# High and low parts of one layer's weights: from engine copies to casting and adding transfers

## The chip, the core and the metric

The kernel runs on one core of a Trainium2 chip. Five engines work beside each other, each through its own list of instructions in order: TensorE (PE in the profile, PEld for its weight loads), VectorE (DVE), ScalarE (ACT), GpSimd (POOL) and SyncE (SP), which here only starts DMA transfers. Semaphores hold an instruction back until what it needs is done. The metric is the device time of one execution in microseconds.

## The reference

A trunk of two layers on x of 512 tokens by 1024 channels, float32. Each layer adds a mixer's output to x and then a squared-ReLU MLP's.

```python
def reference(x, ...):
    for layer in range(2):
        h = rmsnorm(x, norm_mix_g[layer])
        if layer % 2 == 0:
            mix = even_mixer(h, ...)   # S5 state space + dilated window attention
        else:
            mix = mlstm_mixer(h, ...)
        x = x + mix
        h = rmsnorm(x, norm_mlp_g[layer])
        x = x + jnp.square(jax.nn.relu(h @ mlp_w1[layer])) @ mlp_w2[layer]
    return x

def even_mixer(h, w_in, ..., w_glu, q_g, k_g, w_out):
    proj = h @ w_in                       # 1024 x 2048: u, q, k, v of 512 each
    y_a = s5_mixer(u, ..., w_glu)         # ends in y * sigmoid(y @ w_glu), 512 x 512
    y_b = dilated_attention(rotary(rmsnorm(q)), rotary(rmsnorm(k)), v)
    return concatenate([y_a, y_b]) @ w_out   # 1024 x 1024
```

## The kernel before

Products with weights are taken in the type float32r, whose mantissa is shorter than that of float32. To keep the accuracy, both factors are split: a high part, which is the number cast to float32r, and a low part, the rest, also cast. Each product is then three matmuls, high by high, high by low and low by high (`mm3`, line 172). Activations are split by `prep` and the like, weights by the functions below.

All weights come as units of 128 x 1024 numbers (512 KB), in the order of use (`unit_list`, line 1271). Units 0 to 25 belong to the even layer: 0 to 15 are the input projection (four each of u, v and the two kinds of q and k steps), 16 and 17 the S5 gate, 18 to 25 the output projection (`out_proj`, line 424). From unit 26 on come the first MLP, the odd layer and the second MLP; some of these units are sums that `t_sums` makes on the way. A unit feeds 24 matmuls with 512 columns.

`w_next` hands out unit `wi` and calls `w_pump` before and after. `w_pump` starts the raw load of up to three units ahead by SP (`w_dma`, tile `wr`, three buffers) and splits up to two ahead: ACT copies raw to high (`wh`, line 160), DVE subtracts high from raw to give low (`wl`, line 161). There are two pairs of high and low buffers. When the even layer's pools are closed, a further pool `wp2` opens (line 1262), with a third pair, and both distances grow by one.

The even layer follows a list of steps written out by hand (`EVEN_SEQ`, line 30): u, v, a, b are projections, n and r norm and rotary of q and k, C, K, E, T, B, O, G parts of the S5 layer for one of four groups, h attention steps, X and Y the end of S5 and the gate. `s5_params` (line 488) first makes tables on DVE, with 26 and more small products by Pool (line 543, tiles `rA`, `s_pr`, `s_la` ...). Pool also takes a power for each q or k norm (line 800) and starts eight transfers a group that spread S5 matrices into the tile `DT` (line 678). A list scheduler then reorders the whole within what the data and the buffers allow, so the order on an engine differs from that of the code.

The lines that hold a unit's way before the change are these; the functions stand in full below.

```python
self.copy_act(h, r)                  # ACT: high part, cast by the output's type
self.sub(l, r, h.bitcast(F32))       # DVE: low part
```

Of the kernel before, what the change touches and what calls it, by code (L numbers as in the profile page):

```python
# [9 lines left out]
F32 = mybir.dt.float32  # L10
F32R = mybir.dt.float32r
I32 = mybir.dt.int32
AF = mybir.ActivationFunctionType
ALU = mybir.AluOpType
AX = mybir.AxisListType

P = 128
# [44 lines left out]
class Trunk:  # L62
# [67 lines left out]
            self.nc.sync.dma_start(out=self.dbg[name], in_=ap)  # L130


    AHEAD_DMA = 3
    AHEAD_SPLIT = 2
    RAW_BUFS = 3
    MORE_DMA = 1

    def w_init(self, units):
        self.wp2 = None
        self.units, self.wi, self.wd, self.wsx = units, 0, 0, 0  # L140
        self.raw, self.split = {}, {}

    def w_dma(self, n):
        while self.wd < n:
            r = self.t(self.wp, (P, 1024), "wr", F32, self.RAW_BUFS)
            u = self.units[self.wd]
            self.dma(r, u() if callable(u) else u)
            self.raw[self.wd] = r
            self.wd += 1

    def w_pump(self):
        n = 0 if self.wp2 is None else 1
        self.w_dma(min(self.wi + self.AHEAD_DMA + n * self.MORE_DMA, len(self.units)))
        while self.wsx < min(self.wi + self.AHEAD_SPLIT + n, len(self.units)):
            r = self.raw.pop(self.wsx)
            third = self.wp2 is not None and self.wsx % 3 == 2
            pool, bufs = (self.wp2, 1) if third else (self.wp, 2)
            h = self.t(pool, (P, 1024), "wh", F32R, bufs)
            l = self.t(pool, (P, 1024), "wl", F32R, bufs)
            self.copy_act(h, r)  # L160
            self.sub(l, r, h.bitcast(F32))
            self.split[self.wsx] = (h, l)
            self.wsx += 1

# [1060 lines left out]
    def run(self):  # L1225
        nc = self.nc
        a = self.a
        self.x = [None] * KT
        self.prm = self.c((P, 3, 32), "prm")
        self.dma(self.prm, a["s5_par"])  # L1230
        self.x_load([0])
        self.gain = self.c((P, 4, KT), "gain")
        self.w_init(self.unit_list())
        self.w_dma(1)
        self.dma(self.gain, a["gain"])
        self.x_load(range(1, 5))
        cst = self.c((P, P + 24), "cst")
        self.dma(cst, a["cst"])
        self.x_load(range(5, 8))
        self.ident, self.onec, self.bones, self.sgn = cst[:, 0:P], cst[:, P:P + 1], cst[:, P + 1:P + 5], cst[:, P + 5:P + 6]  # L1240
        self.hm, self.eye = cst[:, P + 6:P + 8], cst[:, P + 8:P + 24]
        self.w_dma(2)
        self.s5d = self.c((P, 4, 2), "s5d")
        self.dma(self.s5d, a["s5d"])
        qkg = self.c((P, 4), "qkg")
        self.dma(qkg, a["qkg"])
        rot = self.c((P, 2, T), "rot")
        self.dma(rot, a["rot"])
        self.cos, self.sin = rot[:, 0], rot[:, 1]
        self.ts(qkg[:, 0:2], qkg[:, 0:2], 0.125, ALU.mult)  # L1250
        self.qkg = qkg
        self.pwh = self.c((P, 4, 4), "pwh")
        nc.gpsimd.memset(self.pwh, -0.5)
        self.dp = self.ctx.enter_context(self.tc.tile_pool(name="dp", bufs=1, space=bass.MemoryType.DRAM))
        self.hp = self.ctx.enter_context(self.tc.tile_pool(name="hp", bufs=1))
        self.hg = [None] * KT
        self.tq = {}

        self.even()
        if self.stop == "l0mix":  # L1260
            return self.finish()
        self.wp2 = self.ctx.enter_context(self.tc.tile_pool(name="wp2", bufs=1))
        self.mlp(0)
        if self.stop == "l0":
            return self.finish()
        self.odd()
        if self.stop == "l1mix":
            return self.finish()
        self.mlp(1)
# [129 lines left out]
```

## Time and profile before

| | |
|---|---|
| median of 3 runs | 1186.29 us (1185.99 to 1187.22) |
| profiled execution | 1185.93 us, span 1184.1 us |
| PE busy | 1161.5 us, 98% |
| DVE, ACT, POOL busy | 813.4, 643.1, 64.1 us |
| granted TensorE clock | 0.995 of 2.4 GHz in the mean |
| DMA | 216.56 MB, mean 183 GB/s |

The span runs from the first instruction to the last; the profiled execution's own time is 1.83 us longer. A busy PE may hold pipelined matmuls: one of 512 columns shows about 0.39 us, while the next starts 0.23 us after it. What counts is the stretches in which PE waits, and what ended them.

### The profile page before, as it was taken

What the parts mean: (1) busy time and instruction counts of PE and PEld (TensorE: products, weight loads), DVE (VectorE), ACT (ScalarE), POOL (GpSimd) and SP (SyncE); (2) the same over time, 40 slices, a digit from 0 to 9 for tenths busy, and PEclk for the clock granted to TensorE, in tenths of its full rate; (3) what the DMA queues carried; (4) which work ended last, traced back from release to release, by engine and by line L of the source; (5) the groups of instructions that cost most, each with busy time, mean ns of one, the idle gap of its engine ahead of it and who ended that gap; (6) DMA issues with size and microseconds to landing.
All of it is one profiled execution on the core that took longest, in us unless ns stands there. A gap on an engine that the chain in (4) does not pass through costs nothing.

```text
span 1184.1 us, 15701 instructions
## 1 busy us (share of the span) xinstructions
PE 1161.5 (98%) x5540; PEld 956.2 (81%) x5540; DVE 813.4 (69%) x1466; ACT 643.1 (54%) x1162; POOL 64.1 (5%) x121
## 2 busy tenths in 40 slices
PE   6989999999999999999999999999999999999998
PEld 5868776788888888888888888887888888888887
DVE  8799864666457447779858975865664574477796
ACT  5467777444434446666656645544444444456664
POOL 0522220000000000000100000000000000000000
PEclk9989999999999999999999999999999999999999
DMA  6434531359999335565624333222599994346654
GB/s 236 125 95 122 143 79 58 121 202 370 351 345 357 122 120 160 194 195 172 188 90 153 107 108 107 81 89 72 182 353 367 345 350 144 111 157 195 208 185 158
DMA packets 73869, 216.56 MB, mean 183 GB/s; under 512 B 16888, under 2 KB 17992, under 8 KB 73792
## 3 DMA queue, kind: packets, MB, share of 16 engines
q1 hardware_dynamic: 72576, 214.27, 53.7%
q0 software_dynamic: 1216, 1.31, 0.5%
q8 instruction: 43, 0.70, 0.2%
q14 instruction: 34, 0.28, 0.1%
HBM read 175.14 MB, written 38.31 MB: 180 GB/s over the span
## 4 chain that ended last, share of the span: by engine, by line
PE 92%; DVE 3%; ACT 1%; POOL 1%; issue 1%; DMA 1%; SPq 0%; DVEq 0%; ACTq 0%
PE acc L123 79%; PE psa L123 8%; PE psb L123 3%; DVE wl L96 1%; PE psb L898 1%; POOL rA L543 1%; PE psb L281 1%; ACT wh L120 0%; ACT hg L117 0%; DVE hg L108 0%; DMA hg<-in_amask 0%; DMA wr<-in_w_l 0%; DVE x L108 0%; PE psb L1207 0%; DVE x L96 0%
## 5 line engine op out<-in xcount | busy, mean ns | idle before, releaser
L123 PE MATMUL acc<-hg,wh 128*128 128x512 f32 x1600 | 500.7, 393 | 8.8 <-ACT hg L117 7.2
L120 ACT ACTIVATE wh<-wr 128x1024 fp32r<-128x1024 f32 x243 | 257.2, 1060 | 398.1 <-PE acc L123 321.3
L96 DVE TENSOR_TENSOR wl<-wr,wh 128x1024 fp32r<-128x1024 f32 x243 | 297.3, 1224 | 221.5 <-ACT wh L120 211.4
L123 PEld LDWEIGHTS acc<-hg,wh 128*128 128x128 f32 x1600 | 298.7, 188 | 70.1 <-ACT hg L117 7.2
L123 PE MATMUL acc<-hg,wl 128*128 128x512 f32 x800 | 313.6, 392 | 0.6 <-DVE wl L96 0.6
L123 PE MATMUL acc<-wh,sp 128*128 128x512 f32 x768 | 223.0, 389 | 0.0
L123 PEld LDWEIGHTS acc<-hg,wl 128*128 128x128 f32 x800 | 150.7, 188 | 31.9 <-DVE wl L96 1.1
L123 PEld LDWEIGHTS acc<-wh,sp 128*128 128x128 f32 x768 | 144.2, 188 | 30.0
L123 PE MATMUL acc<-wl,sp 128*128 128x512 f32 x384 | 135.9, 390 | 0.8 <-DVE wl L96 0.8
L120 ACT ACTIVATE sp<-s 128x256 fp32r<-128x256 f32 x224 | 89.8, 409 | 6.8 <-PE acc L123 5.7
L96 DVE TENSOR_TENSOR tq<-tq,tq 128x1024 f32<-128x1024 f32 x64 | 78.2, 1222 | 21.0 <-DMA tq<-in_w2s 20.0
L96 DVE TENSOR_TENSOR sp<-s,sp 128x256 fp32r<-128x256 f32 x224 | 86.8, 417 | 1.4 <-ACT sp L120 1.4
L123 PEld LDWEIGHTS acc<-wl,sp 128*128 128x128 f32 x384 | 71.9, 188 | 16.6 <-DVE wl L96 1.6
L123 PE MATMUL acc<-wh,hg 128*128 128x512 f32 x192 | 63.0, 402 | 5.4 <-ACT wh L120 5.4
L123 PEld LDWEIGHTS acc<-wh,hg 128*128 128x128 f32 x192 | 36.6, 193 | 13.2 <-ACT wh L120 5.8
L123 PE MATMUL psa<-wh,sp 128*128 128x512 f32 x128 | 42.0, 389 | 0.0
L117 ACT ACTIVATE rr<-acc 128x512 f32<-128x512 f32 x72 | 41.6, 578 | 0.0
L117 ACT ACTIVATE s<-rr 128x512 f32<-128x512 f32 x64 | 40.4, 631 | 1.0
L123 PE MATMUL acc<-wl,hg 128*128 128x512 f32 x96 | 38.5, 401 | 0.3 <-DVE wl L96 0.3
L108 DVE SCALAR_TENSOR_TENSOR sf<-zb,cvw,sf 128x512 f32<-128x512 f32 x48 | 35.3, 747 | 2.3 <-ACT sf L117 1.8
L96 DVE TENSOR_TENSOR x<-x,acc 128x512 f32<-128x512 f32 x16 | 10.8, 686 | 29.3 <-PE acc L123 29.2
L123 PE MATMUL acc<-y,wh 128*128 128x512 f32 x96 | 30.0, 394 | 0.0
(324 smaller groups left out, 1327.7 us busy)
## 6 DMA issues: line engine op xcount, KB each, us to landing
wr<-in_w_l SPq DMA_DIRECT2D x67, 512.0 KB, 3.5
wr<-in_w SPq DMA_DIRECT2D x64, 512.0 KB, 5.2
tq<-in_w2s SPq DMA_DIRECT2D x64, 512.0 KB, 6.3
T<-tq SPq DMA_DIRECT2D x64, 512.0 KB, 4.8
wr<-T SPq DMA_DIRECT2D x64, 512.0 KB, 3.3
wr<-in_w2s SPq DMA_DIRECT2D x48, 512.0 KB, 4.0
x<-in_xT SPq DMA_DIRECT2D x16, 256.0 KB, 4.1
na<-scr SPq DMA_DIRECT2D x8, 256.0 KB, 3.7
```

Of the source, the lines that this page charges most:

```text
L96: return self.nc.vector.tensor_tensor(out=o, in0=x, in1=y, op=op)
L108: return self.nc.vector.scalar_tensor_tensor(out=o, in0=x, scalar=s, in1=y, op0=op0, op1=op1)
L117: return self.nc.scalar.activation(o, x, f, bias=bias, scale=scale, **kw)
L120: return self.nc.scalar.activation(o, x, AF.Copy)
L123: return self.nc.tensor.matmul(o, l, r, start=start, stop=stop)
L281: self.nc.tensor.transpose(p[:, k * P:(k + 1) * P], self.x[4 * n + k][:, t * P:(t + 1) * P], self.ident)
L543: gt = lambda o, x, y, op: self.nc.gpsimd.tensor_tensor(out=o, in0=x, in1=y, op=op)
L898: self.nc.tensor.transpose(t[:, k * P:(k + 1) * P], p[:, k * P:(k + 1) * P], self.ident)
```

## The change

For units 0 to 25 no raw tile is loaded. Pool starts a casting transfer from the weights in HBM to the high tile (float32 to float32r). When it has landed, ACT writes the negated high part into the low tile. Then Pool starts a second transfer of the same weights, which adds to the low tile: raw minus high. High and low tiles have three buffers in one pool, and units are prepared up to three ahead. From unit 26 on everything is made as before, with raw tiles of which one buffer lies in the old pool and two in `wp2`; `w_pump` touches these units only when `wp2` is open (one raw tile, of unit 27, has its place before that).

```diff
-    AHEAD_DMA = 3
-    AHEAD_SPLIT = 2
-    RAW_BUFS = 3
-    MORE_DMA = 1
+    AHEAD = 3
+    BY_DMA = 26
 
     def w_init(self, units):
         self.wp2 = None
-        self.units, self.wi, self.wd, self.wsx = units, 0, 0, 0
+        self.units, self.wi, self.wd, self.wsx = units, 0, self.BY_DMA, 0
         self.raw, self.split = {}, {}
 
     def w_dma(self, n):
         while self.wd < n:
-            r = self.t(self.wp, (P, 1024), "wr", F32, self.RAW_BUFS)
+            second = self.wd % 3 > 0
+            r = self.t(self.wp2 if second else self.wp, (P, 1024), "wr", F32, 2 if second else 1)
             u = self.units[self.wd]
 ...
     def w_pump(self):
-        n = 0 if self.wp2 is None else 1
-        self.w_dma(min(self.wi + self.AHEAD_DMA + n * self.MORE_DMA, len(self.units)))
-        while self.wsx < min(self.wi + self.AHEAD_SPLIT + n, len(self.units)):
-            r = self.raw.pop(self.wsx)
-            third = self.wp2 is not None and self.wsx % 3 == 2
-            pool, bufs = (self.wp2, 1) if third else (self.wp, 2)
-            h = self.t(pool, (P, 1024), "wh", F32R, bufs)
-            l = self.t(pool, (P, 1024), "wl", F32R, bufs)
-            self.copy_act(h, r)
-            self.sub(l, r, h.bitcast(F32))
+        if self.wp2 is not None:
+            self.w_dma(min(self.wi + self.AHEAD + 1, len(self.units)))
+        while self.wsx < min(self.wi + self.AHEAD, len(self.units)):
+            if self.wsx >= self.BY_DMA and self.wp2 is None:
+                break
+            h = self.t(self.wp, (P, 1024), "wh", F32R, 3)
+            l = self.t(self.wp, (P, 1024), "wl", F32R, 3)
+            if self.wsx < self.BY_DMA:
+                u = self.units[self.wsx]
+                self.nc.gpsimd.dma_start(out=h, in_=u)
+                self.act(l, h.bitcast(F32), AF.Copy, scale=-1.0)
+                self.nc.gpsimd.dma_start(out=l, in_=u, accum_op=ALU.add)
+            else:
+                r = self.raw.pop(self.wsx)
+                self.copy_act(h, r)
+                self.sub(l, r, h.bitcast(F32))
             self.split[self.wsx] = (h, l)
             self.wsx += 1
 ...
         self.w_init(self.unit_list())
-        self.w_dma(1)
+        self.w_pump()
 ...
-        self.w_dma(2)
```

What the scheduler makes of it is seen in three places. In these rows a bracket names the semaphores that an instruction waits for (PE_49 is PE's count, DMASW0_49 one of eight counts of Pool's transfers, DMAHW those of SP's).

First, PE at the start. `acc` is the sum of a projection, `hg` the split activations; the first number of a weight tile tells units apart. Before:

```order
L123 MATMUL acc_50_339<-hg_28_128,wh_52_342 128x512 [waits Activation_49]
L123 MATMUL acc_50_339<-hg_28_128,wh_52_342 128x512 [waits DVE_49]
L123 MATMUL acc_50_339<-hg_28_128,wl_53_343 128x512
L123 MATMUL acc_50_339<-hg_28_128,wh_52_342 128x512 [waits Activation_49]
L123 MATMUL acc_50_339<-hg_28_128,wh_52_342 128x512 [waits DVE_49]
```

Now:

```order
L123 MATMUL acc_54_350<-hg_32_139,wh_4_72 128x512 [waits DMASW0_49,Activation_49]
L123 MATMUL acc_74_439<-hg_32_139,wh_6_77 128x512 [waits DMASW1_49]
L123 MATMUL acc_54_350<-hg_32_139,wh_4_72 128x512 [waits DVE_49]
L123 MATMUL acc_74_439<-hg_32_139,wh_6_77 128x512
L123 MATMUL acc_91_528<-hg_32_139,wh_8_82 128x512 [waits DMASW2_49]
L123 MATMUL acc_91_528<-hg_32_139,wh_8_82 128x512
L123 MATMUL acc_54_350<-hg_32_139,wl_5_73 128x512 [waits DMASW3_49]
L123 MATMUL acc_54_350<-hg_32_139,wh_4_72 128x512 [waits Activation_49]
```

Two matmuls each of units 0, 1 and 2 on high parts now stand ahead of the first one on a low part (`wl_5_73`).

Second, Pool amid the S5 tables (`pr` and `pis` are powers of a rotation). Before:

```order
L543 TENSOR_TENSOR s5_pr_43_272<-rA_34_153 128x32 [waits Pool_49]
L543 TENSOR_TENSOR rA_34_153<-rA_34_153 128x32 [waits Pool_49]
L543 TENSOR_TENSOR s5_pis_44_273<-rA_34_153 128x32 [waits Pool_49]
L543 TENSOR_TENSOR rA_34_153<-s5_pr_43_272 128x32 [waits Pool_49]
L543 TENSOR_TENSOR rA_34_153<-s5_pis_44_273 128x32
L543 TENSOR_TENSOR s5_pr_43_272<-rA_34_153 128x32 [waits Pool_49]
L543 TENSOR_TENSOR rA_34_153<-s5_pr_43_272,s5_pis_44_273 128x32 [waits Pool_49]
L543 TENSOR_TENSOR s5_pis_44_273<-rA_34_153 128x32 [waits Pool_49]
L543 TENSOR_TENSOR rA_34_153<-s5_pr_43_272 128x32 [waits Pool_49]
```

Now:

```order
L548 TENSOR_TENSOR s5_pr_47_283<-rA_38_164 128x32 [waits Pool_49]
L548 TENSOR_TENSOR rA_38_164<-rA_38_164 128x32 [waits Pool_49]
L548 TENSOR_TENSOR s5_pis_48_284<-rA_38_164 128x32 [waits Pool_49]
L548 TENSOR_TENSOR rA_38_164<-s5_pr_47_283 128x32 [waits Pool_49]
L548 TENSOR_TENSOR rA_38_164<-s5_pis_48_284 128x32
L548 TENSOR_TENSOR s5_pr_47_283<-rA_38_164 128x32 [waits Pool_49]
L162 DMA wl_76_441<-in_w_l0 128x1024 [waits DMASW4_49,PE_49,Activation_49]
L548 TENSOR_TENSOR rA_38_164<-s5_pr_47_283,s5_pis_48_284 128x32 [waits Pool_49]
L160 DMA wh_92_529<-in_w_l0 128x1024 [waits DMASW2_49,PE_49]
L548 TENSOR_TENSOR s5_pis_48_284<-rA_38_164 128x32 [waits Pool_49]
L548 TENSOR_TENSOR rA_38_164<-s5_pr_47_283 128x32 [waits Pool_49]
```

The adding transfer of unit 4 (`wl_76`) and the casting transfer of unit 5 (`wh_92`) stand in the middle of the S5 operations. So do those of units 6 to 10 further on, among the other operations of line 543 (now 548), the power of line 800 (now 805) and the eight transfers of line 678 (now 683).

Third, SP between the even layer and the MLP (`in_w1` holds the MLP's first matrix, `in_w2s` its second; `tq` are tiles of `t_sums`). Before:

```order
L126 DMA wr_521_2340<-in_w_l0 128x1024 [waits DMAHW0_49,DVE_49]
L126 DMA wr_526_2377<-in_w_l0 128x1024 [waits DMAHW1_49,DVE_49]
L126 DMA wr_531_2414<-in_w_l0 128x1024 [waits DMAHW2_49,DVE_49]
L126 DMA wr_536_2451<-in_w1 128x1024 [waits DMAHW3_49,DMAHW0_49,DVE_49]
L126 DMA wr_541_2488<-in_w1 128x1024 [waits DMAHW4_49,DMAHW1_49,DVE_49]
L126 DMA wr_546_2525<-in_w1 128x1024 [waits DMAHW5_49,DMAHW2_49,DVE_49]
L126 DMA wr_551_2571<-in_w1 128x1024 [waits DMAHW6_49,DMAHW3_49,DVE_49]
```

Now:

```order
L126 DMA x1_476_2206<-in_xT 128x512 [waits DMAHW7_49,DVE_49]
L126 DMA x2_477_2208<-in_xT 128x512 [waits DMAHW1_49,DMAHW0_49,DVE_49]
L126 DMA x3_478_2210<-in_xT 128x512 [waits DMAHW3_49,DVE_49]
L126 DMA wr_518_2531<-in_w1 128x1024 [waits DVE_49,PE_49]
L126 DMA wr_520_2535<-in_w1 128x1024
```

The MLP's first load (`wr_518`, unit 26) no longer follows a subtraction of a unit before; it waits for a count of PE, that of the last but one block of the output projection's last unit.

## Rows read from the trace of the kernel before

**Rows 1.** Page: span, and busy time of each engine.

```profile
span 1184.1 us, 15701 instructions
...
PE 1161.5 (98%) x5540; PEld 956.2 (81%) x5540; DVE 813.4 (69%) x1466; ACT 643.1 (54%) x1162; POOL 64.1 (5%) x121
```

**Rows 2.** Windows by stage: length, busy (count) of PE, PEld, DVE, ACT, POOL; clock.

```profile
0.00:17.64 17.64, 8.74 (x27) 6.06 (x27) 13.90 (x43) 13.62 (x22) 2.09 (x7) 1.00 0.85 306
...
59.79:67.91 8.12, 2.46 (x6) 1.16 (x4) 7.96 (x22) 4.95 (x10) 3.29 (x2) 0.73 0.19 65
67.91:134.26 66.35, 66.35 (x407) 57.50 (x407) 64.44 (x149) 46.67 (x91) 12.03 (x17) 0.98 0.45 129
...
147.00:208.90 61.90, 60.48 (x358) 43.08 (x357) 36.09 (x92) 45.98 (x108) 8.46 (x16) 1.00 0.25 68
...
253.30:1184.10 930.80, 924.99 (x4277) 768.93 (x4275) 619.88 (x980) 483.49 (x832) 14.72 (x36) 1.00 0.58 200
```

**Rows 3.** Waits of PE, 0 to 400 us: total, times, longest.

```profile
PE acc L123 <- ACT wh L120: 5.4, 1, 5.4
```

**Rows 4.** Timeline of PE, 16 to 75 us: start, length, what [idle before].

```profile
65.57 2.07 PE L123 MATMUL acc<-wh,hg 128*128 128x512 f32 x4 [5.39 <-ACT wh L120]
67.91 0.79 PE L123 MATMUL acc<-wl,hg 128*128 128x512 f32 x1 [0.27 <-DVE wl L96]
...
70.51 0.39 PE L123 MATMUL acc<-wl,hg 128*128 128x512 f32 x1
```

**Rows 5.** Chain of waits, 0 to 400 us: start, length, what.

```profile
220.97 43.36 PE acc L123 x190
264.33 0.79 PE psb L123 x8
265.12 0.50 PE psb L281 x4
```

**Rows 6.** Timeline of POOL: start, length, what [idle before].

```profile
38.15 0.43 POOL L543 TENSOR_TENSOR rA<-rA 128x32 f32<-128x32 f32 x2 [35.53 <-DVE sf L96]
...
41.69 0.53 POOL L543 TENSOR_TENSOR s_pr<-rA 128x32 f32<-128x32 f32 x1
...
59.08 3.16 POOL L800 TENSOR_TENSOR qky<-qkv,pwh 128x16 f32<-128x16 f32 x1 [1.43 <-DVE qkv L108]
62.22 0.86 POOL L543 TENSOR_TENSOR s_lb<-s_lb,rB 128x288 f32<-128x288 f32 x1
80.68 4.54 POOL L678 DMA_DIRECT2D DT<-dk  x8 [17.60 <-DMA dk<-y]
```

**Rows 7.** DVE by line, 0 to 260 us, and the page's row on ACT.

```profile
L96 DVE TENSOR_TENSOR wl<-wr,wh 128x1024 fp32r<-128x1024 f32 x29 | 35.9, 1242 | 7.5 <-ACT wh L120 7.4
...
L120 ACT ACTIVATE wh<-wr 128x1024 fp32r<-128x1024 f32 x243 | 257.2, 1060 | 398.1 <-PE acc L123 321.3
```

**Rows 8.** Tile DT: its issues (ns), and the time to landing.

```profile
L678 POOL DMA_DIRECT2D DT<-dk x32: 533/591/742, 80.7 to 155.9; - x32
...
DMA to landing us min/median/max: 2.0/2.5/4.1
```

**Rows 9.** Tile wr: its loads.

```profile
DMA to landing us min/median/max: 3.1/3.5/8.5
```

**Rows 10.** DMA, 0 to 40 us, in 40 slices of 1 us.

```profile
GB/s 0 17 182 322 362 281 393 381 405 404 432 354 414 401 414 379 252 0 82 291 180 188 315 0 0 0 193 332 0 16 0 0 115 315 102 0 0 37 221 266
```

**Rows 11.** Windows of the subtractions alone: length, DVE busy (count), clock.

```profile
0.00:38.15 38.15, 7.33 (x6) 1.00 0.59 199
```

**Rows 12.** Timelines of SP and of all engines around the transition.

```profile
233.90 16.65 SPq L126 DMA_DIRECT2D wr<-in_w  x4
...
250.22 0.33 SPq L126 DMA_DIRECT2D wr<-in_w  x1
...
253.29 0.61 PE L123 MATMUL acc<-hg,wh 128*128 128x512 f32 x2
...
253.61 2.01 ACT L120 ACTIVATE wh<-wr 128x1024 fp32r<-128x1024 f32 x2 [3.54 <-DMA wr<-in_w]
```

## Prediction

> **What bounds the kernel now.** I read the page's head first: TensorE (PE) is busy in 98% of the span, so only places where PE stands still, or runs slowly, can give time back [rows 1]. The profiled execution took 1185.93 us, 1.83 above its span; the median of the three runs is 1186.29, 0.36 more. Then I cut the span by stage with the windows view [rows 2]. The even layer, the only one whose 26 weight units change, ends at 253.3 us; from there to the end PE has 924.99 of 930.80 us. The order of every engine behind the first MLP blocks is the same in both programs, so what counts is when the MLP starts.
>
> PE's waits in the first 400 us name one long one behind the start: 5.4 us, before 65.57 us, ended by ACT's high copy [rows 3, 4]. It costs more than its length: from 67.91 to 70.51 us six matmuls start, one per 0.433 us, where 190 in a row take 0.228 each at the full level (43.36/190) [rows 4, 5]. So the granted clock falls to its lower level, 1.2 GHz, behind that idle; the 0.73 granted in 59.79 to 67.91 says the same [rows 2]. About ten matmuls at 0.205 too much are 2.1 us. Idle 5.4, a further 0.3 for the low part, and 2.1: **7.8 us** is all that this place can return. The chain behind it runs through Pool's S5 operations (38.15 to 63.1 us) and DVE, which is busy in 7.96 of the 8.12 us [rows 2, 6].
>
> **What goes and what comes.** DVE loses 26 subtractions of 1.24 us, 32 us [rows 7]. ACT keeps one pass a unit: a negating copy of 128x1024 in place of a plain one, taken at the same 1.06 us [rows 7]; both are ACTIVATE of one size, so I see neither gain nor loss. SP loses 26 issues. Pool gets 52, at 0.59 us each by its DT issues [rows 8]: 31 us on an engine that is busy for 64 [rows 1]. As throughput all of it is hidden; what isn't hidden is latency and Pool's order.
>
> A weight unit is 24 matmuls, 5.47 us. There are three buffers, so a unit is refilled from the end of its predecessor by three, and two units, 10.9 us, cover this. Before, the raw load ran ahead in buffers of its own, and only 1.06 and 1.24 us lay between a freed buffer and a ready unit. Now the whole chain lies there: casting transfer h, ACT's 1.06, adding transfer l, and about 0.3 of hand-overs. Nothing in the trace casts or adds. The nearest rows are plain loads of the same 512 KB: 3.1 to 8.5 us, median 3.5 [rows 9]. Pool's own transfers, of 64 KB or less, land in 2.0 to 4.1 [rows 8]. I take h = 4.0, near the median, and l = 5.0, since the adding one also reads its destination; both ends, 3.5 and 8.5, stay for the range (a cheaper one than a plain load is excluded: it moves no fewer bytes). The loop is 0.3 + 4.0 + 1.06 + 5.0 = 10.4 us: just covered where nobody is late, late wherever Pool is held.
>
> **Start.** PE's order now runs six matmuls on high parts of units 0 to 2, then needs the first low part. Ahead of that on the wire lie eight x tiles (2.1 MB) and three casts (1.6 MB); with its own 0.5 MB this is 4.2 MB at about 0.4 MB per us from 1.7 us on [rows 10]: 12.3, and with a tail of 1.7 it lands at 14. Before, 27 matmuls were done at 17.64 [rows 2, 4]. The 21 that are missing take 4.9 us at the lower level (as after 65.57) for eleven, and ten at 0.228: PE is there at 21.2, **+3.6**. (At 10 us instead of 14 it would be -0.4, at 18 +7.6.)
>
> **Pool's order, first 90 us.** The DVE chain that feeds S5 loses six subtractions, 7.3 us [rows 11], so Pool may start at 30.8 instead of 38.15, and the 7.8 us wait goes: **-7.8**. What is late next are low parts that stand behind other work on Pool, which goes strictly in order:
> - Unit 4: its adding transfer stands behind eleven S5 operations (4.1 us in before, 38.15 to 42.2 [rows 6]), so it goes out at 35 and lands at 40; PE wants it at 39.1, its third matmul. 1.0 late.
> - Unit 5: behind seventeen more operations (6.2 us) and the cast of unit 6, which waits for PE to leave unit 3 (38.6): out at 44.3, lands 49.3; wanted at 46.9. 2.4 late.
> - Unit 7: its cast stands behind the 3.16 us power [rows 6] and three 0.9 us products, out at 54.2; negated at 59.4, low part lands at 64.5; wanted at 60.2. 4.3 late.
> - Unit 9: held by the cast of unit 10, which waits for PE to leave unit 7; about 20 small matmuls lie between. 0.
> - Unit 10: behind eight DT transfers (4.54 us [rows 6]) that wait for dk, out at 79.9, lands 84.9; wanted at 83.1. 1.8 late.
>
> Together **+9.5**. Behind these I find three units or many small matmuls between refill and use: 0. In attention (147 to 208.9) DVE works 36.09 of 61.9 us and PE is full [rows 2]: nothing to win, 0.
>
> **Output projection.** Units 18 to 20 are in place. If unit 18 ends at T, 21's cast lands at T+4.1 and its low part at T+10.4. PE has units 19 and 20 and four matmuls until T+7.3: **+3.1**. The next four refill in 10.4 against 10.9: 0 more.
>
> **Into the MLP.** Before, four MLP loads went out from 233.9 on, and PE went from one stage to the other without a gap at 253.29 [rows 12]. Now raw tiles of units 26 and 28 lie in a pool that opens only when the even layer's tiles are done: the load waits for PE's last block but one, 0.6 us before the end. A load took 3.4 us there (250.22 to 253.61), the high copy 1.06 [rows 12, 7], so PE stands 4.0 us and then pays the lower level, 2.1; norm and transposes of 1.3 us slip into the gap [rows 5]. **+4.8**.
>
> **Sum.** 3.6 - 7.8 + 9.5 + 3.1 + 4.8 = +13.2, on 1185.93: **1199**.
>
> **Rivals.**
> *Transfers at the plain price.* With h = l = 3.5 the loop is 8.4. The first low part comes at 12 (+1.6), units 4 to 10 lose 0, 0.9, 2.3, 0.3, the projection 0.6, the MLP 4.8: 1.6 - 7.8 + 3.5 + 0.6 + 4.8 = +2.7, 1189. For it: the median of the same size. Against: loads in the first 40 us took longer, and an add has more to do. In the Trainium skill, "DMA: Bandwidth & Descriptors", section "Anatomy of one DMA — SWDGE (gpsimd) path", a transfer issued by Pool costs about 2.0 us plus its bytes at 436 GB/s, so 3.2 us for one of these (an estimate by that page); the plain 3.5 agrees with it, and by it this rival would be the forecast. It says nothing of casts or adds.
> *DVE's relief decides: faster.* If low parts come to Pool's places in time (a loop under about 6 us, or a Pool that reaches its DMAs earlier than I work out) and the first lands at 10, then -0.4 - 7.8 + 0 + 0 + 4.8 = -3.4, 1182.5. It turns at the point where the five stalls above sum to less than 3.4 us. For it: DVE is full from 60 to 134 us. Against: h and l would each have to beat every load of this size.
> *The adding transfer is slow.* With l = 8.5, the slowest landing of such a load, the loop is 13.9 and cover runs out by 3.0 at each turn of three buffers: start +3.5, +3.5 more at unit 4, 5, 7 and 10, and 3.5 more at three places of the projection: 13.2 + 28 = +41 at most; as one wait shifts the next, I take two thirds of it, +28: 1214. The slow end of both is beyond it. The same section family of that page ("SWDGE vs HWDGE vs iDMA") says that descriptors are written to SBUF by Pool and that DVE can shut it out meanwhile. Eight issues at 80.68 us took 4.54 us [rows 6] while DVE was busy in 64.44 of 66.35 us [rows 2], so no row bears it out; it would only add to this case.
> That the subtractions stay is excluded: in the new order DVE has none before the MLP.
>
> **Chances.** Forecast (1193 to 1205) 0.44, plain price 0.2, DVE's relief 0.12, slow add 0.24. A kernel like this is told from no change beyond 0.2%, 2.4 us: faster is the relief, 0.12; half of the plain-price case falls within, 0.10; slower 0.78. The range for 8 in 10 runs from 1186 to 1222.
>
> **What would show it.** Right: PE's wait before 65 us gone or ended by a DMA of wl; waits of PE for wl's DMA at the third matmul of units 4, 5, 7 and 10 and of the fourth projection unit; 4 us of PE idle ahead of the MLP, ended by ACT's wh; everything behind shifted by one constant. Wrong: landings of wl under 4 us, PE without waits from 20 to 90 us, or an MLP that starts before 253.3.

## The result and the profile after

The changed kernel takes 1229.27 us (median of 4 runs, 1227.69 to 1231.62), the kernel before 1186.76 beside it: a ratio of 1.036, 95% interval 1.0338 to 1.0382. Forecast were 1199, with 1186 to 1222: the direction was right, the size was not, and the time lies outside the range.

The page of the changed kernel (head; packets, MB and engine share of Pool's queue; DMA issues with KB each and the median of the time to landing in us):

```profile
span 1229.0 us, 15718 instructions
...
PE 1180.0 (96%) x5540; PEld 965.7 (79%) x5540; DVE 791.0 (64%) x1440; ACT 644.8 (52%) x1162; POOL 99.4 (8%) x173
...
q0 software_dynamic: 8704, 28.58, 10.6%
...
wh<-in_w_l POOLq DMA_DIRECT2D x26, 512.0 KB, 4.9
wl<-in_w_l POOLq DMA_DIRECT2D x26, 512.0 KB, 5.9
```

The DMA view of its first 297 us has the transfers that the S5 layer sends through HBM and back, in the same columns:

```profile
bin<-in_s_bc SPq DMA_DIRECT2D x4, 256.0 KB, 7.5
dl<-x SPq DMA_DIRECT2D x4, 256.0 KB, 6.4
...
x<-du SPq DMA_DIRECT2D x4, 256.0 KB, 4.2
```

Against [rows 1] PE is busy for 18.5 us more, though it does the same 5540 matmuls: it ran slower in places. A casting transfer lands after 4.9 us in the median, an adding one after 5.9; assumed were 4.0 and 5.0. The 26 loads that they replace took 3.8; the 3.5 that the prediction went by is the median of all the kernel's loads into `wr` [rows 9]. The S5 layer's transfers are later too: `bin` took 4.5 before, `dl` 2.6, `x<-du` 2.8.

The windows view, cut where the MLP begins (columns as in [rows 2]):

```profile
0.00:297.34 297.34, 254.32 (x1276) 197.09 (x1277) 172.55 (x463) 162.32 (x333) 84.76 (x137) 0.94 0.61 148
297.34:1229.00 931.66, 925.71 (x4266) 768.61 (x4264) 618.42 (x978) 482.50 (x830) 14.62 (x36) 1.00 0.58 200
```

From the MLP on the two kernels are alike, 931.66 us against 930.80 [rows 2]. The MLP starts at 297.34 in place of 253.29, so 44.05 of the 44.9 us between the two spans lie ahead of it, as the prediction had assumed. PE stands still there for 43.0 us (297.34 less 254.32), before for 16.8 (253.3 less the 236.5 that [rows 1] and [rows 2] leave for the even layer). Where it does, by PE's timeline (start, length, what, and the idle time ahead of it with what ended it):

```profile
15.49 0.80 PE L123 MATMUL acc<-hg,wl 128*128 128x512 f32 x1 [3.52 <-DMA wl<-in_w_l]
...
38.55 0.50 PE L123 MATMUL acc<-hg,wl 128*128 128x512 f32 x1 [1.47 <-DMA wl<-in_w_l]
...
46.71 0.50 PE L123 MATMUL acc<-hg,wl 128*128 128x512 f32 x1 [1.51 <-DMA wl<-in_w_l]
...
59.43 0.80 PE L123 MATMUL acc<-hg,wl 128*128 128x512 f32 x1 [4.65 <-DMA wl<-in_w_l]
...
75.73 0.80 PE L123 MATMUL acc<-wl,hg 128*128 128x512 f32 x1 [2.56 <-DMA wl<-in_w_l]
...
91.98 1.79 PE L123 MATMUL psa<-U,BT 128*128 128x64 f32 x8 [4.27 <-ACT BT L120]
...
166.33 1.65 PE L123 MATMUL psa<-k,hg 128*128 128x384 f32 x2 [3.13 <-DVE nm L886]
...
259.21 0.60 PE L123 MATMUL acc<-y,wl 128*128 128x512 f32 x1 [2.94 <-DMA wl<-in_w_l]
...
278.00 0.50 PE L123 MATMUL acc<-y,wl 128*128 128x512 f32 x1 [1.01 <-DMA wl<-in_w_l]
...
286.07 0.50 PE L123 MATMUL acc<-y,wl 128*128 128x512 f32 x1 [2.34 <-DMA wl<-in_w_l]
...
295.87 1.05 PE L123 MATMUL psb<-cst,ss 128*128 128x1 f32 x8 [2.92 <-DVE ss L96]
```

The wait of 5.4 us before 65.57 [rows 4] is gone, and nine others over 1.4 us stand in its place behind the start: six for an adding transfer, those for `BT` and `nm` from the chains of S5 and attention, and the one ahead of the MLP. In the view of PE's waits (us in total, times, longest) the adding transfers lead:

```profile
PE acc L123 <- DMA wl<-in_w_l: 20.2, 9, 4.6
```

The rest of the time is the clock. These windows are the stretches at its lower level (PE's busy time is the second number, the granted clock the third from the end):

```profile
58.00:65.00 7.00, 5.57 (x13) 4.41 (x14) 3.88 (x12) 5.46 (x13) 4.00 (x5) 0.51 0.66 162
...
75.00:82.00 7.00, 6.27 (x15) 4.93 (x16) 5.85 (x17) 4.01 (x8) 0.00 (x0) 0.51 0.67 183
...
92.00:96.00 4.00, 4.00 (x15) 3.53 (x16) 3.96 (x10) 2.11 (x5) 4.00 (x8) 0.57 0.23 63
...
126.00:134.00 8.00, 7.77 (x26) 6.11 (x26) 3.21 (x7) 5.90 (x8) 3.80 (x2) 0.57 0.85 189
...
163.00:171.00 8.00, 4.39 (x12) 1.68 (x15) 2.20 (x10) 6.30 (x13) 4.93 (x2) 0.57 0.37 130
...
258.00:263.00 5.00, 3.79 (x10) 2.98 (x11) 0.56 (x1) 1.06 (x1) 0.34 (x1) 0.66 0.96 218
...
286.00:291.00 5.00, 4.93 (x15) 3.91 (x16) 0.15 (x1) 0.00 (x0) 0.00 (x0) 0.66 0.00 0
...
297.00:301.00 4.00, 4.00 (x14) 3.14 (x13) 3.83 (x6) 2.52 (x4) 0.00 (x0) 0.57 1.00 396
```

In each, by estimate, PE loses its busy time times what is missing from 1: 2.7, 3.1, 1.7, 3.3, 1.9, 1.3, 1.7 and 1.7, together 17.4 us (before: 2.3 behind 65.57, and 1.7 at 138 to 142). Seven of the eight stand behind a wait of 2.3 us or more; the one at 126 to 134 stands behind some 30 matmuls of 4 to 64 columns without a wait (PE's only wait there, 0.23 us, ends at 129.12, after the fall). Behind the two waits of 1.5 us the level stayed up.

### The profile page after: what moved, and what is told of

Read it like the earlier page. It is cut to its first block, busy times and chain, and to the rows that moved or that the text cites. A ratio compares the mean times of both kernels' runs of the same rounds, so it can differ in the third digit from the quotient of the medians.

```text
span 1229.0 us, 15718 instructions
## 1 busy us (share of the span) xinstructions
PE 1180.0 (96%) x5540; PEld 965.7 (79%) x5540; DVE 791.0 (64%) x1440; ACT 644.8 (52%) x1162; POOL 99.4 (8%) x173
## 3 DMA queue, kind: packets, MB, share of 16 engines
q0 software_dynamic: 8704, 28.58, 10.6%
## 4 chain that ended last, share of the span: by engine, by line
PE 83%; DMA 6%; issue 6%; ACT 2%; DVE 2%; POOL 1%; SPq 0%; DVEq 0%; POOLq 0%; ACTq 0%
PE acc L123 72%; PE psa L123 7%; DMA wl<-in_w_l 3%; PE psb L123 2%; DMA wh<-in_w_l 2%; DMA bin<-in_s_bc 1%; DMA cst<-in_cst 1%; PE psb L903 1%; PE psb L286 1%; POOL wh L160 0%; ACT hg L117 0%; DVE wl L96 0%; ACT wl L117 0%; POOL wl L162 0%; DVE x L108 0%
## 5 line engine op out<-in xcount | busy, mean ns | idle before, releaser
L123 PE MATMUL acc<-hg,wh 128*128 128x512 f32 x1600 | 507.5, 398 | 9.4 <-ACT hg L117 7.3
L120 ACT ACTIVATE wh<-wr 128x1024 fp32r<-128x1024 f32 x217 | 229.7, 1060 | 352.0 <-PE acc L123 297.9
L96 DVE TENSOR_TENSOR wl<-wr,wh 128x1024 fp32r<-128x1024 f32 x217 | 265.2, 1223 | 198.4 <-ACT wh L120 194.0
L123 PEld LDWEIGHTS acc<-hg,wh 128*128 128x128 f32 x1600 | 302.3, 191 | 72.5 <-ACT hg L117 7.3
L96 DVE TENSOR_TENSOR tq<-tq,tq 128x1024 f32<-128x1024 f32 x64 | 78.2, 1222 | 39.2 <-DMA tq<-in_w2s 35.8
L117 ACT ACTIVATE wl<-wh 128x1024 fp32r<-128x1024 f32 x26 | 27.5, 1057 | 44.1 <-DMA wh<-in_w_l 34.5
L117 ACT ACTIVATE hg<-x,gain 128x512 fp32r<-128x512 f32 x32 | 23.0, 718 | 26.7 <-DVE x L96 23.7
```

The source lines that it names most:

```text
L96: return self.nc.vector.tensor_tensor(out=o, in0=x, in1=y, op=op)
L117: return self.nc.scalar.activation(o, x, f, bias=bias, scale=scale, **kw)
L120: return self.nc.scalar.activation(o, x, AF.Copy)
L123: return self.nc.tensor.matmul(o, l, r, start=start, stop=stop)
```

## Experiments

Each ratio is to the kernel before, which took 1186.6 to 1187.2 us beside these runs. No version beat it.

**A plain low transfer.** In the changed kernel:

```diff
-                self.nc.gpsimd.dma_start(out=l, in_=u, accum_op=ALU.add)
+                self.nc.gpsimd.dma_start(out=l, in_=u)
```

> The changed kernel, with the adding transfer made a plain one of the same 512 KB from Pool (so the low tile holds the whole weight, and the output is not the reference's); the order of all engines is the same. Theory add (the adding is what is dear, since it also reads its destination): the landing of wl falls from a median of 5.9 us to the 4.9 of wh, the waits of PE for wl (20.2 us in 9) to about 11, some of the lower clock behind them goes too: 1215 to 1219 us. Rival queue (what Pool starts is dear by itself, whatever it does at its destination): wl stays above 5.5 and the time within 3 us of 1229.

Measured: 1210.57 us, ratio 1.0200 (1.0176 to 1.0224): 18.7 us less, more than the theory had asked for. Pool's queue and transfers by its page, S5's by its DMA view, and PE's waits, as above:

```profile
q0 software_dynamic: 8704, 28.58, 7.8%
...
wh<-in_w_l POOLq DMA_DIRECT2D x26, 512.0 KB, 4.3
wl<-in_w_l POOLq DMA_DIRECT2D x26, 512.0 KB, 4.3
```

```profile
bin<-in_s_bc SPq DMA_DIRECT2D x4, 256.0 KB, 5.0
dl<-x SPq DMA_DIRECT2D x4, 256.0 KB, 4.3
```

```profile
PE acc L123 <- DMA wl<-in_w_l: 6.0, 4, 2.0
```

Low parts land after 4.3 us in place of 5.9 (shortest 3.7 in place of 5.3), PE's waits for them fall from 20.2 to 6.0 us. It is the adding that is dear. And it is dear for others: the packets of Pool's queue took 7.8% of 16 engines over 1208.9 us, 1509 us of engine time, with the adding 10.6% over 1229.0, 2084. The difference is 22 us a transfer, or 1.4 us of all sixteen engines, and casts, `bin` and `dl` land 0.6 to 2.5 us earlier without it. As nothing else was changed, not even the order, this is shown.

**Both in the same form.** As above, with the source of both transfers named as float32r:

```diff
-                self.nc.gpsimd.dma_start(out=h, in_=u)
+                self.nc.gpsimd.dma_start(out=h, in_=u.bitcast(F32R))
...
-                self.nc.gpsimd.dma_start(out=l, in_=u, accum_op=ALU.add)
+                self.nc.gpsimd.dma_start(out=l, in_=u.bitcast(F32R))
```

> As the run with a plain low transfer, and the casting transfer also made a plain copy of the bits (output not the reference's). Theory cast: the landing of wh falls from 4.9 us towards the 3.5 of SP's loads, the time falls by 10 us or more against the run with a plain low transfer. Rival queue: wh stays at 4.5 or more, the time within 3 us of that run.

Measured: 1211.83 us (ratio 1.0208, 1.0191 to 1.0226), high parts after 4.7 us, low ones after 4.0. No difference, as the rival said. The run says less than it was meant to: a transfer from float32r to float32r may be handled as a cast as well, and then nothing was taken away. What bounds the cast's price is the run with raw loads by Pool, further on, as far as two kernels with other traffic can be compared.

**The MLP's first units early.** In the changed kernel, `w_dma` takes a raw tile from the old pool until `wp2` is open, and `w_pump` no longer stops at unit 26:

```diff
-            second = self.wd % 3 > 0
+            second = self.wp2 is not None and self.wd % 3 > 0
...
-            if self.wsx >= self.BY_DMA and self.wp2 is None:
-                break
+            self.w_dma(max(self.wd, self.wsx + 1))
```

> The changed kernel, with the raw tiles of units 26 to 28 loaded and split before the even layer's tiles are given back (one raw buffer in the old pool until then). Theory transition (the late first load of the MLP costs 4.8 us, as predicted): 1224 to 1225 us, no idle of PE over 1 us at the start of the MLP, no lower clock there. Rival norm (the 2.9 us of idle there was ended by DVE's sum of squares, not by a weight, so the norm would be late anyway): 1228 to 1230.

Measured: 1223.87 us (runs from 1217.93 to 1226.45), ratio 1.0318 (1.0301 to 1.0335), 5.4 less than the changed kernel by the medians; from the last matmul of the output projection to the first of the MLP it is 0.23 us in place of 4.8, with no lower clock behind. Theory transition holds at its place; the spread of the runs leaves the size open by some us. That DVE's sum of squares ended the wait in the changed kernel only told what came last there: this order puts the sum ahead of the MLP, since its weights are late anyway.

**The output projection by the engines.** The same code with

```diff
-    BY_DMA = range(26)
+    BY_DMA = range(18)
```

> As the run with the early MLP, and units 18 to 25 (the output projection) made by the engines again, by one raw buffer. Theory lateness: the three waits of the output projection (2.9, 1.0 and 2.3 us) and the lower clock behind two of them (1.6 and 1.7 us) go as well: 9.5 us below the run with the early MLP, 1214 to 1216. Rival raw: with one raw buffer load and split take about 6.3 us a unit against 5.47 of PE, and PE waits as long: within 3 us of the run with the early MLP.

Measured: 1210.38 us, ratio 1.0204 (1.0186 to 1.0223): 13.5 less than with all 26 units by the medians, 8.0 by the two traced executions (1218.22 and 1210.24), where 9.5 were expected. The projection's waits and the lower clock behind them are gone, so theory lateness holds, though the size is known only roughly; one raw buffer was enough.

**Both transfers at once, no copy.** As the first experiment, with ACT's negating copy left out too:

```diff
-                self.act(l, h.bitcast(F32), AF.Copy, scale=-1.0)
-                self.nc.gpsimd.dma_start(out=l, in_=u, accum_op=ALU.add)
+                self.nc.gpsimd.dma_start(out=l, in_=u)
```

> The run with a plain low transfer, and ACT's negating copy left out, so that both transfers of a unit go out together and neither ACT nor the second transfer waits for the first (output not the reference's; the order of the engines differs in places). Theory chain (what is left is the row cast, copy, second transfer, and ACT and Pool standing at instructions that wait for it): PE's waits for wl, for BT (3.2 us) and for nm (3.0 us) go, with the lower clock behind them; left are the start and the MLP's 4.8 us, and the old stall of 7.8 us is gone: 1185 to 1192 us. Rival Pool (52 transfers started by Pool are dear in themselves): 1203 or more.

Measured: 1200.56 us, ratio 1.0117 (1.0099 to 1.0135), between the two. PE's waits for `wl` are down to 0.5 us, those for `BT` and `nm` are gone. But a new one of 7.6 us stands at 116. The chain of waits into it (start, length, what):

```profile
99.90 3.60 DMA du<-x
...
103.57 8.18 DMA x<-du
...
111.81 1.28 ACT L117
...
114.70 0.53 ACT y L120
...
115.86 0.17 DVE qkv L108
...
116.08 1.11 PE psb L653 x4
```

`x<-du`, a transfer of 256 KB that took 2.8 us before, took 8.18: it ran beside the four transfers of two units, 2 MB, that Pool sent off between 101.25 and 104.2. DVE then stood at `y`, with `qkv` behind it.

**Raw loads by Pool.** In the kernel before:

```diff
-            self.dma(r, u() if callable(u) else u)
+            (self.nc.gpsimd if self.wd < 26 else self.nc.sync).dma_start(out=r, in_=u() if callable(u) else u)
```

> The kernel before, with the 26 plain raw loads of the even layer started by Pool in place of SP. Theory chain: a raw tile is loaded three units ahead, so a landing of about 4.3 us and Pool's other work are hidden: 1185 to 1190 us. Rival Pool (its queue and its landing decide): PE waits for raw tiles amid the S5 operations, 1195 or more.

Measured: 1203.57 us, ratio 1.0141 (1.0114 to 1.0168): the rival's side. The landing is not the reason (4.0 us in the median, 3.8 by SP). Pool goes in order, and a load now stands ahead of the S5 operations, which start at 42.10 in place of 38.15 [rows 6]:

```profile
40.68 0.53 POOL L147 DMA_DIRECT2D wr<-in_w_l  x1 [7.43 <-DVE qv L96]
42.10 0.43 POOL L543 TENSOR_TENSOR rA<-rA 128x32 f32<-128x32 f32 x2 [0.89 <-DVE sf L96]
```

But behind the load Pool waits another 0.89 us for DVE's `sf`, so the load by itself does not explain the later start; what does is not shown. A plain load by Pool at 4.0 and a cast at 4.3 to 4.9, in kernels with different traffic beside them, put what casting adds at under 1 us in the median.

**Pool subtracts.** In the kernel before:

```diff
-            self.sub(l, r, h.bitcast(F32))
+            if self.wsx < 6:
+                self.nc.gpsimd.tensor_tensor(out=l, in0=r, in1=h.bitcast(F32), op=ALU.subtract)
+            else:
+                self.sub(l, r, h.bitcast(F32))
```

> The kernel before, with the subtractions of units 0 to 5 by Pool in place of DVE. Pool took 0.86 to 1.1 us for 128x288, so an estimate of 3.1 to 3.9 us for 128x1024. Theory relief (DVE's load ahead of the S5 operations makes the 5.4 us wait and the lower clock behind it): six times 1.24 us come off DVE, the wait goes or shrinks to under 2 us: 1178 to 1183. Rival Pool hold (the S5 operations then wait for Pool's subtractions): the wait stays or moves, 1185 to 1195.

Measured: 1198.27 us, ratio 1.0092 (1.0076 to 1.0108). The theory fell; the wait moved, as the rival said, but the time lies above the rival's range too. Two rows of Pool's timeline, a subtraction and the first S5 operation:

```profile
32.17 2.40 POOL L162 TENSOR_TENSOR wl<-wr,wh 128x1024 fp32r<-128x1024 f32 x1 [7.42 <-ACT wh L120]
38.38 0.82 POOL L546 TENSOR_TENSOR rA<-rA 128x32 f32<-128x32 f32 x2 [3.82 <-DVE sf L96]
```

A subtraction takes 2.4 to 2.9 us, less than estimated, but S5 starts at 38.38 and not a moment earlier, though DVE was rid of four of the six by then: up to 38.15 us it is as busy as before (33.06 us against 32.77), since the new order has other work in their place. The wait of 5.4 us comes again as one of 4.84, at 73.14, and new ones of 2.8 and 3.3 us stand at 19.09 and 147.24.

**A filled wait.** In the kernel before (`zero` is a tile of zeros):

```diff
+        if u == 2:
+            for n in range(16):
+                self.mm(accs[n % 4], self.zero, acts[0][0], False, False)
```

> The kernel before, with 16 more matmuls of 512 columns ahead of the unit that PE waits 5.4 us for (their left factor is zero, so they add nothing to the sums; the order differs a little behind them). Theory clock (the lower level behind a wait comes of PE standing idle): the wait is still ended by ACT's copy at about 65.6 us, but shrinks to about 1.7 us, and the matmuls behind it come every 0.228 us: 2 us off, 1184. Rival (the lower level there comes whatever PE did before): matmuls at 0.433 us as before, 1186 to 1188.

Measured: 1202.12 us, ratio 1.0124 (1.0108 to 1.0140). At the place itself the theory has its way: the wait shrinks to 1.82 us, and the four matmuls behind it take 1.20 us in place of 2.07 [rows 4].

```profile
60.02 3.83 PE L123 MATMUL acc<-hg,zero 128*128 128x512 f32 x16
...
65.67 1.20 PE L123 MATMUL acc<-wh,hg 128*128 128x512 f32 x4 [1.82 <-ACT wh L120]
```

The level falls a little later all the same (0.66 in 67 to 72 us), behind a second wait of 1.16. What the 16 matmuls cost lies elsewhere: the order planned around them is another one, with new waits of 2.1 and 1.6 us in the even layer and 7.3 us more from the MLP on.

**Casts a unit earlier.** In the changed kernel, a fourth buffer for high parts in the place of the raw tile:

```diff
+        while self.hx < min(self.wi + self.AHEAD + 1, self.BY_DMA):
+            h = self.t(self.wp, (P, 1024), "wr", F32R, 1) if self.hx % 4 == 3 else self.t(self.wp, (P, 1024), "wh", F32R, 3)
+            self.nc.gpsimd.dma_start(out=h, in_=self.units[self.hx])
+            self.high[self.hx] = h
+            self.hx += 1
...
-            h = self.t(self.wp, (P, 1024), "wh", F32R, 3)
+            h = self.high.pop(self.wsx) if self.wsx < self.BY_DMA else self.t(self.wp, (P, 1024), "wh", F32R, 3)
...
-                self.nc.gpsimd.dma_start(out=h, in_=u)
...
```

> The changed kernel, with a fourth buffer for high parts (the raw tile's place, free in the even layer), so that a unit's cast goes out one unit earlier than its adding transfer and ACT need it. Theory late (the row of cast, copy and adding transfer is too long for the 10.9 us of cover): what is left behind a freed low tile is 0.3 + 1.06 + 5.9 = 7.3 us; PE's waits for wl behind the start and ACT's waits for casts ahead of BT and nm go, with most of the lower clock: 1190 to 1202 us; the start (6 us) and the MLP's 4.8 stay. Rival Pool order (casts and adds stand behind Pool's other work, wherever the buffers would let them go): waits for wl of 8 us or more in sum behind the start, 1212 or more.

Measured: 1221.85 us, ratio 1.0295 (1.0271 to 1.0319). Half of theory late holds: the waits for `wl` behind the start come to 4.3 us, and those for `BT` and `nm` are gone; yet the time is on the rival's side. Another wait takes their place:

```profile
133.51 1.09 PE L657 MATMUL psb<-cst,Z 128*128 128x128 f32 x4 [8.04 <-DVE Z L96]
```

The chain into it runs through `du` and `x<-du` again, which land after 6.3 and 8.1 us there; adding transfers take 6.6 in the median. That the work which comes earlier collides on the DMA engines is argued from these times; no run took it apart. And with

```diff
-    BY_DMA = 26
+    BY_DMA = 29
```

> As the run with the early cast, and units 26 to 28 of the MLP also made by casting and adding transfers, so that the MLP's first weights need no new buffer. Theory transition: the 2.9 us of idle and the lower clock ahead of the MLP go, 4 to 5 us below the run with the early cast. Rival: the last transfers are late there too, within 2 us of that run.

it is 1219.27 us (ratio 1.0270, 1.0250 to 1.0290): 2.6 less where 4 to 5 were expected, with intervals that overlap, so it decides nothing; the same wait is there, with 8.2 us.

**No transfer at all.** The code of the run with the early MLP, with `BY_DMA = range(0)`:

> A control: the run with the output projection by the engines, and units 0 to 17 by the engines too: no casting or adding transfer at all, but the buffers of the changed kernel (three pairs of high and low parts, one raw tile until the MLP) and an order planned anew. Theory transfers (what is left in the run with units 0 to 17 by transfers, 1210 us, comes of these transfers): 1184 to 1194 us. Rival plan (the even layer loses as much whenever its buffers and its order change, as the three runs with a changed kernel before did with 1198 to 1204): 1198 or more.

Measured: 1203.74 us, ratio 1.0142 (1.0125 to 1.0159): rival plan. The old wait is there with 6.3 us in place of 5.4; PE's row at the largest new wait, and the windows behind it:

```profile
136.79 2.08 PE L123 MATMUL psb<-cst,rr 128*128 128x128 f32 x8 [4.69 <-ACT BT L120]
```

```profile
137.00:145.00 8.00, 8.00 (x39) 8.00 (x39) 6.09 (x9) 2.70 (x5) 0.00 (x0) 0.50 0.23 79
145.00:153.00 8.00, 8.00 (x38) 8.00 (x38) 6.12 (x11) 3.79 (x7) 0.00 (x0) 0.50 0.39 102
153.00:160.00 7.00, 7.00 (x23) 5.08 (x23) 4.86 (x16) 4.64 (x10) 4.65 (x2) 0.50 0.15 33
```

ACT waits for the one raw tile (1.8 us before 132.03) ahead of `BT` in its order, which explains that much of the 4.69 at most; and the clock then stays at its lower level for 23 us, with PE busy all through. So a change of buffers and order costs the even layer 17 us without a single casting or adding transfer. Order and buffers were not told apart.

## Why the prediction was wrong

By the prediction's own steps, in us (the wait and the clock of each place from the rows above, less what the same stretch lost before):

| step | forecast | measured |
|---|---|---|
| start | +3.6 | +6.0 |
| wait before 65.57 goes | -7.8 | -7.9 |
| late low parts and other waits, 24 to 255 us | +9.5 | +30.3 (19.2 waits, 11.1 clock) |
| output projection | +3.1 | +9.2 (6.2 waits, 3.0 clock) |
| into the MLP | +4.8 | +4.9 |
| sum | +13.2 | +42.5 of 44.9 |

*Right.* The old wait is gone; the MLP's late load cost what was worked out, and the run that loads it early gave 5.4 us back; the fourth unit of the projection waited 2.94 us where 3.1 were forecast; all behind is shifted by one constant. (The 7.3 us of PE's work ahead of that unit are less than the two whole units that the prediction names, 10.9 us, since PE's order begins units 19 and 20 before 18 is done; in the run it was about 7.7.)

*Start.* The 28th matmul starts at 23.93 us in place of 17.97 (the 17.64 of the prediction is the start of the 27th). The first low part came at 15.49, not 14, and PE then had a dozen matmuls to do at the lower level, and two short waits of 0.6 us together.

*The step that failed* is "Pool's order, first 90 us", with the loop of 10.4 us under it, in three ways.

First, "l = 5.0" was under the shortest adding transfer of the run, 5.3: a read of the destination was allowed for, but not what it does to the engines. The loop came to 0.3 + 4.9 + 1.06 + 5.9 = 12.2 us against a cover of 10.9; it was forecast as just covered, so that only Pool's other work made parts late. It is late by itself, and in the projection, where Pool has little else to do, that gives the waits of 1.01 and 2.34 us that the prediction put at 0. In the first 90 us the idle time in sum, 10.2 us, is near the 9.5 forecast, but partly by luck. By the order in which the transfers land PE waits for units 3, 4, 5 and 7 (1.47, 1.51, 4.65 and 2.56 us); forecast were 4, 5, 7 and 10 (1.0, 2.4, 4.3 and 1.8). And ahead of units 4 and 5 it is not the S5 operations that hold Pool. The chain of waits into the longest, before 59.43 (start, length, what):

```profile
32.64 7.12 DMA wh<-in_w_l
...
39.78 1.07 ACT wl L117
...
41.77 0.20 POOL rA L548
41.97 7.65 DMA wh<-in_w_l
...
49.64 1.07 ACT wl L117
...
51.00 8.39 DMA wl<-in_w_l
```

Two casts of more than 7 us and an adding transfer of 8.4, with one S5 operation of 0.20 between them: the cast of unit 5 stands behind the adding transfer of unit 4 on Pool, which waits for ACT's copy of a cast that is late. In the run with a plain low transfer, in the same order, these three took 4.88, 5.58 and 4.94 us, and from 24 to 60 us PE waited for no low part. That run prices the adding as a whole, start and clock included, at 18.7 us. The Trainium skill's estimate for a transfer by Pool, 3.2 us by "DMA: Bandwidth & Descriptors", section "Anatomy of one DMA — SWDGE (gpsimd) path", is near the shortest cast (3.7) and far from every adding one. In the run with raw loads by Pool a plain one took 4.0 in the median. So no row of the changed kernel bears out the rival at the plain price.

Second, each late low part was put down by its idle time alone, with no clock behind it, though the prediction had priced exactly this at the old wait (2.1 us) and at the MLP. Behind late low parts it cost 8.8 us: 5.8 in the middle (58 to 65 and 75 to 82) and 3.0 in the projection.

Third, "behind these I find ... 0" looked for weights alone. Waits for `BT` (4.3 us) and `nm` (3.1, and 0.5 for the `hg` behind it) with the clock behind them, 11.5 together, come from the S5 and attention chains, whose own transfers land later beside Pool's and whose places in the order are new. In the chain into `BT` the transfer `bin` takes 5.36 us (from 84.13) and ACT's negating copy 1.06; ahead of `nm` DVE waits 3.54 us for ACT, which stood 2.58 for `x<-du`. The rest of the clock in the middle, 1.7 us more than the same stretch lost before, fell at 126 to 134 behind short matmuls.

*The rivals.* DVE's relief decided nothing: S5 started at 34.77 in place of the 30.8 worked out, and when six subtractions alone were taken off DVE it did not start earlier at all. So whether this relief removed the old wait is not shown: ACT's copy to `wh`, for which PE waited there [rows 4], has no place in the new program. The slow add was the rival with the right mechanism, and it named three waits in the projection, as there were: 1214 by two thirds of its 41 us, and the whole of it, 1227, comes near the measured time, but its transfers took 5.9 and not 8.5 us in the median; that the sum comes near is luck, since the clock and the waits for `BT` and `nm`, which it did not have, made up the rest.

*Open.* How much of the 42 us the new order would cost by itself. The control with no transfers loses 17, three kernels with a small change to the one before lose 11 to 17, but each by waits of its own, so none of them says what share the changed kernel has. The rows are of one execution, and those of one kernel differ: 4 us between the runs of the changed kernel, 8.5 with the MLP's first units early.

## What to carry to other kernels

A transfer that adds into its destination is not a load with a copy saved: here it landed 1.6 us later in the median than the same transfer without the adding, and the transfers beside it landed 0.6 to 2.5 us later too. Where a refill turns from one hop into several in a row, compare the row of hops with the cover of the buffers, at medians of the very kind of transfer; where the kind is not in the trace, run it before trusting a price. Put PE's lower clock behind a wait into the sum (here by estimate 1.3 to 3.1 us behind each wait of 2.3 us or more), and do not take an order worked out for other costs or buffers as free: the four kernels here that changed them without a casting or adding transfer lost 11 to 17 us, each by waits of its own.

## What the runs showed of the hardware that was not expected

- One adding transfer of 512 KB from HBM took 22 us of DMA engine time more than a casting one, 1.4 us of all sixteen.
- The granted clock fell without an idle PE: at 126 to 134 us of the changed kernel, behind some 30 matmuls of 4 to 64 columns. And in the control it stayed at half from 137 to 160 us, behind a wait of 4.69, with PE busy in all of these 23 us, all with matmuls of 384 columns or fewer.
- Pool's subtraction of 128x1024 took 2.4 to 2.9 us, about twice DVE's 1.24 [rows 7].
